# Depthwise convolution: the taps of two of eight channel groups as ScalarE products and GpSimd sums; all input products of the second block in three parts

## The chip, the cores and the metric

One Trainium2 chip, of which the program uses one core. The metric is the device time of one execution in microseconds (us). The engines of the core go by these names: PE is TensorE (PEld its weight loads), DVE is VectorE, ACT is ScalarE, POOL is GpSimd, SP is SyncE, which issues the DMAs. Each engine works through its own list of instructions in order and waits on semaphores for the others.

## The reference

The model has two blocks on 256 tokens of 2048 channels, all in fp32. The change lies in the second block, in its convolution branch:

```python
def conv_group(u, conv_dw_w, conv_dw_b, conv_ln_g, conv_ln_b):
    a, gate = jnp.split(u, 2, axis=-1)
    h = a * jax.nn.sigmoid(gate)
    h = lax.conv_general_dilated(
        h, conv_dw_w[:, None, :].astype(h.dtype), window_strides=(1,),
        padding=[(CONV_K - 1, 0)], dimension_numbers=("NWC", "WIO", "NWC"),
        feature_group_count=CONV_CH) + conv_dw_b
    h = layer_norm(h, conv_ln_g, conv_ln_b)
    return jax.nn.silu(h)

def second_block(x, ...):
    xn = rms_norm(x, norm1_g)
    proj = xn @ w_in + b_in
    # conv_in, q, k, v are slices of proj
    conv_out = conv_group(conv_in, ...)
    attn_out = swa_group(q, k, v, ...)
    x = x + jnp.concatenate([conv_out, attn_out], axis=-1) @ w_out
    ...
```

CONV_CH is 1024 and CONV_K is 31: every channel is convolved along the tokens with its own 31 taps. On the chip a channel is a partition, so the 1024 channels are 8 groups of 128, and a group is 31 taps over a tile of 128 x 256.

## The kernel before

The program is one long list in Python order; a scheduler then sets the order on each engine from its own estimate of when things are ready, so instructions of neighbouring steps stand interleaved.

Products with weights are done in three parts. A weight tile of 512 KB (128 x 1024, ring of 4, name `wr`) comes by DMA; ACT writes its rounded copy `wh` (`wsplit`, L422), DVE subtracts that to get the rest `wl` (L423), both in rings of 3; PE then multiplies wh by the high part of the activation, wh by its low part, and wl by its high part (`three`, L456, L459, L460). A group of 256 output columns is four weight tiles, 96 matmuls of 256 columns (`proj`). For the groups in `N32 = (6, 7)`, that is the last two of the eight convolution inputs, `proj32` (L478) is used instead: the weight tile stays in fp32, ACT scales it in 16 pieces of 128 x 256 (L486), and PE multiplies it with the residual `hT` itself in fp32 (L490), 32 matmuls that the trace shows as 64 records.

The order of the stage in the program is: `conv_in(0)` and `conv_in(1)` (product, tanh gate, and the gated input `hp` of a group, L829 to L833), the product for k and v, four products for q, then eight rounds, each with one more `conv_in` (groups 2 to 7 in the first six) and one attention unit (scores `ps_sc`, softmax on DVE and ACT, transposes `ps_pt`, output `ps_o`, result in `mixed`). After each of these steps `tap(n)` takes up to n taps off a list. A tap is one DVE instruction, co = hp shifted by k, times a weight per channel, plus co (L825; the first tap of a group, with the bias, is L823). Then come the output products of the attention half (`out_half(i, 1)`, eight times 48 matmuls `ps_out`; the last two of them are held behind the mean), with the taps that are left and the scaling of `hT` by the last norm (L873) between. The mean over the channels (`ps_mu`, L882) needs all eight groups of co; the layer norm follows, then the convolution half of the output product.

`hp` and `co` are slices of one tile, which the trace calls `cq`. `ag` is the product of a `conv_in` after its scaling (L402), `q_s` that of a q product. POOL has no instruction in this stage; its first are in the top-k that comes later (L971, L1001).

Of the kernel before, what the change touches and what calls it, by code (L numbers as in the profile page):

```python
# [9 lines left out]
F32 = mybir.dt.float32  # L10
# [4 lines left out]
AF = mybir.ActivationFunctionType  # L15
OP = mybir.AluOpType
# [3 lines left out]
P = 128  # L20
T = 256
# [16 lines left out]
UL = 126  # L38
UB = (6, 4)
VPACE, UPACE, UR = False, True, 4  # L40
N32 = (6, 7)
VR, VB, VLAG = 6, 3, 2
TAPS = (20, 20, 6)
CF = 2
# [154 lines left out]
def body(ctx: ExitStack, tc: tile.TileContext, a, out):  # L199
    nc = tc.nc  # L200
    V, S, G, PE = nc.vector, nc.scalar, nc.gpsimd, nc.tensor
# [40 lines left out]
    def right(stack, name, bufs=1):  # L242
        return stack.enter_context(tc.tile_pool(name=name, bufs=bufs, side="right", reuse_waits="tile"))
# [6 lines left out]
    tm = right(p0, "tm", 2)  # L250
# [3 lines left out]
    def const(name, dtype=F32, pool=rc):  # L254
        shape = list(a[name].shape)
        t = pool.tile(shape, dtype, name="c_" + name)
        nc.sync.dma_start(t, a[name])
        return t
# [96 lines left out]
    def cut(t, o, *shape):  # L355
        n = int(np.prod(shape))
        v = t[:, o:o + n]
        return v.rearrange("p (a b) -> p a b", a=shape[0]) if len(shape) == 2 else v

    def tmp(name, tag, dtype=F32):  # L360
        return tm.tile([P, T], dtype, tag=tag, name=name)
# [37 lines left out]
    def scaled(ps, rr, name):  # L399

        t = tm.tile([P, 512], F32, tag="td", name=name, bufs=3)
        V.tensor_tensor(t.rearrange("p (a b) -> p a b", a=2), ps.rearrange("p (a b) -> p a b", a=2),  # L402
                        twice(rr), OP.mult)
        return t

    def scaled2(ps, rr, name):
        t = total(ps, name)
        t3 = t.rearrange("p (a b) -> p a b", a=2)
        V.tensor_tensor(t3, t3, twice(rr), OP.mult)
        return t  # L410
# [233 lines left out]
    for i in range(4):  # L644
# [14 lines left out]
    for i in range(8):  # L659
        gs = []  # L660
        for name, tag, o, act_in in (("ga", "ta", 0, "w_ga"), ("gb", "tb", 16, "w_gb")):
            t = scaled2(proj2(act_in, i, u), r1, name)
# [4 lines left out]
        t = total(proj2("w_oa", i, ab, kt=2), "ya")  # L667
        for j in range(2):
            V.tensor_tensor(gs[j], gs[j], t[:, j * T:(j + 1) * T], OP.mult)
        t = total(proj2("w_ob", i, ab, kt=2, c0=8), "yb")  # L670
# [32 lines left out]
    for i, shift in ((1, 0.0), (0, 0.25)):  # L703
        k = tmp("an_k", "ta")
# [43 lines left out]
    for gi, n in enumerate(GROUPS):  # L748
        f = cut(slot("ff", F32R), 0, 8, 2 * T)
        for i in range(n):  # L750
            ps = scaled2(proj2("w_up", up0 + i, u), r2, "up")
            cs = []
            for j in range(2):
                ch = 44 * j + up0 + i
                s = ps[:, j * T:(j + 1) * T]
                t = tmp("ff_t%d" % j, "t" + "ab"[j])
# [17 lines left out]
    cw_2 = const("cw_2")  # L774
    cb_2 = const("cb_2")
# [7 lines left out]
    hp = cut(cq, 0, 8, T + 30)  # L783
    co = cut(cq, 2288, 8, T)
# [31 lines left out]
    V.memset(hp[:, :, 0:30], 0.0)  # L816
    taps = []

    def tap(n):
        for _ in range(min(n, len(taps))):  # L820
            i, k = taps.pop(0)
            if k == 0:
                V.tensor_scalar(co[:, i], hp[:, i, 0:T], cw_2[:, i, 0:1], cb_2[:, i:i + 1], OP.mult, OP.add)  # L823
            else:
                V.scalar_tensor_tensor(co[:, i], hp[:, i, k:k + T], cw_2[:, i, k:k + 1], co[:, i],  # L825
                                       OP.mult, OP.add)

    def conv_in(i):
        ps = scaled(proj32("w_in2", i, hT, g_both) if i in N32 else proj("w_in2", i, u), r3, "ag")  # L829
        S.activation(ps[:, T:2 * T], ps[:, T:2 * T], AF.Tanh, bias=hb_in2[:, 2 * i + 1:2 * i + 2], scale=0.5)  # L830
        S.activation(ps[:, 0:T], ps[:, 0:T], AF.Identity, bias=hb_in2[:, 2 * i:2 * i + 1], scale=0.5)
        V.scalar_tensor_tensor(hp[:, i, 30:], ps[:, T:2 * T], 1.0, ps[:, 0:T], OP.add, OP.mult)
        taps.extend((i, k) for k in range(31))  # L833

    for i in range(CF):
        conv_in(i)
        tap(TAPS[2])

    src = scaled(proj("w_in2", 8, u), r3, "kv_s")
# [4 lines left out]
    for tt in range(2):  # L844
        PE.transpose(pt[:, tt * P:(tt + 1) * P], vT[:, tt * P:(tt + 1) * P], ident)
    S.activation(vtok[:, :, :P], pt[:, :T].rearrange("p (a b) -> p a b", a=2), AF.Copy)
    tap(TAPS[2])
    for i in range(4):
        src = scaled(proj("w_in2", 9 + i, u), r3, "q_s")
# [21 lines left out]
    for i in range(8):  # L871
# [5 lines left out]
            out_half(i, 1)  # L877
        tap(TAPS[1])
    tap(len(taps))
    pm = ptp.tile([P, 512], F32, tag="tp", name="ps_mu")  # L880
    for c in range(8):
        mean = PE.matmul(pm[:, :T], onesD, co[:, c], start=c == 0, stop=c == 7)  # L882
# [11 lines left out]
    for c in range(8):  # L894
        V.tensor_tensor(co[:, c], co[:, c], r, OP.mult)
        t = tmp("ln_t", "ta")
# [161 lines left out]
    for h in range(8):  # L1058
# [11 lines left out]
        for tt in range(2):  # L1070
            S.activation(sub[:, tt * T:(tt + 1) * T], pk[:, tt * T:(tt + 1) * T], AF.Copy,
                         scale=r4t[:, tt:tt + 1])
# [260 lines left out]
```

## Time and profile before

| | us |
|---|---|
| median of 3 runs | 3003.82 (3000.06 to 3008.96) |
| the profiled execution | 3007.65 |
| its span | 3005.9 |
| PE busy in the span | 2934.2 (98%) |
| DVE busy | 2399.6 (80%) |
| ACT busy | 1570.0 (52%) |
| POOL busy | 857.2 (29%) |

A profile is one execution, taken by the hardware profiler. A busy share is a mean over stages with different limits, so the rows below cut the span into the stretches around the convolution, from 1385 to 1612 us. An instruction's duration holds some time in which the next one already runs, so of a row of equal instructions the time divided by their count is the better price. The idle time in front of a group of instructions is given with the instruction that ended it. PEclk is the granted clock of TensorE, as a share of full speed (2.4 GHz).

### The profile page before, as it was taken

The numbers are of one execution on the slowest core, as the hardware profiler recorded it, in microseconds if no ns is written. First come the engines' busy times: TensorE is split into PE (matmuls) and PEld (weight loads), VectorE is DVE, ScalarE is ACT, GpSimd is POOL, SyncE is SP. The second block draws the span as 40 slices with busy tenths as digits, with TensorE's granted clock in tenths as the row PEclk, the third lists the DMA queues.
The fourth block names the chain that finished last, engine by engine and source line by source line (L and its number), as shares of the span: only waits on it lengthen the run. The fifth ranks groups of instructions, "written<-read, shape, count | busy, mean of one in ns | idle before, by whom it ended". The sixth has DMA issues, their size and how long they took to land.

```text
span 3005.9 us, 49957 instructions
## 1 busy us (share of the span) xinstructions
PE 2934.2 (98%) x18472; PEld 2620.7 (87%) x18472; DVE 2399.6 (80%) x4392; ACT 1570.0 (52%) x2312; POOL 857.2 (29%) x670
## 2 busy tenths in 40 slices
PE   8999999999999999999989989999999999999999
PEld 7888888888888888878979989999999888888887
DVE  6567666777777676778997788999987988999998
ACT  5565555554545454556565535555555554444444
POOL 0000000000000000000000155555554897777776
PEclk9999999999999999999999999999999999999999
DMA  6446565655665656544434679999999338999998
GB/s 222 155 141 185 189 189 189 190 183 189 189 190 189 189 183 195 187 157 155 148 101 151 231 242 316 325 325 323 323 314 317 112 139 319 331 336 333 332 340 311
DMA packets 211142, 686.35 MB, mean 228 GB/s; under 512 B 29264, under 2 KB 47056, under 8 KB 210512
## 3 DMA queue, kind: packets, MB, share of 16 engines
q1 hardware_dynamic: 169776, 523.15, 52.8%
q0 software_dynamic: 41120, 160.01, 15.6%
q8 instruction: 144, 2.36, 0.3%
q14 instruction: 102, 0.84, 0.1%
HBM read 677.41 MB, written 5.64 MB: 227 GB/s over the span
## 4 chain that ended last, share of the span: by engine, by line
PE 71%; DVE 9%; issue 7%; POOL 7%; DMA 4%; ACT 2%; POOLq 0%; DVEq 0%; SPq 0%; ACTq 0%
PE ps_w_up L443 11%; PE ps_w_up L445 6%; PE ps_dn L443 5%; POOL vrows L1020 5%; PE ps_u L460 3%; PE ps_u L456 3%; PE ps_u L459 3%; DMA urows<-in_u_rows,ex 3%; PE ps_dn L445 3%; PE y L1305 2%; PE y L1304 2%; PE y L1303 2%; PE ps_w_ga L443 2%; PE ps_w_cv L443 2%; PE ps_w_gb L443 2%
## 5 line engine op out<-in xcount | busy, mean ns | idle before, releaser
L423 DVE TENSOR_TENSOR wl<-wr,wh 128x1024 fp32r<-128x1024 f32 x572 | 699.9, 1225 | 358.4 <-ACT wh L422 357.8
L422 ACT ACTIVATE wh<-wr 128x1024 fp32r<-128x1024 f32 x572 | 605.3, 1059 | 672.7 <-PE ps_dn L443 117.8
L971 POOL TENSOR_TENSOR tk_c<-tk_v 128x256 f32<-128x256 f32 x16 | 12.1, 758 | 1714.8 <-DVE tk_v L963 1714.4
L1020 POOL DMA_INDIRECT vrows<-in_v_rows,ex x256 | 382.9, 1496 | 134.7 <-DVE yg L1272 74.8
L460 PE MATMUL ps_u<-u_a,ul 128*128 128x256 f32 x1408 | 401.2, 285 | 15.5 <-DVE ul L423 14.1
L459 PE MATMUL ps_u<-u_a,uh 128*128 128x256 f32 x1408 | 397.8, 283 | 0.0
L456 PE MATMUL ps_u<-u_a,uh 128*128 128x256 f32 x1408 | 397.7, 282 | 0.0
L422 ACT ACTIVATE uh<-ur 128x512 fp32r<-128x512 f32 (+1 forms) x384 | 226.2, 597 | 240.5 <-DMA ur<-in_u_dense 86.7
L443 PE MATMUL ps_w_up<-u_a,wh 128*128 128x512 f32 x968 | 342.8, 393 | 0.0
L1020 POOL DMA_INDIRECT urows<-in_u_rows,ex x228 | 268.4, 1177 | 213.3 <-PE ps_u L460 129.7
L1288 ACT ACTIVATE vhi<-vraw 128x1472 fp32r<-128x1472 f32 x128 | 184.0, 1438 | 264.4 <-PE y L1305 252.5
L1305 PE MATMUL y<-vhi,al 128*128 128x512 f32 (+1 forms) x768 | 298.5, 389 | 0.7 <-DVE al L1296 0.5
L1303 PE MATMUL y<-vhi,ah 128*128 128x512 f32 (+1 forms) x768 | 295.3, 385 | 3.5 <-ACT ah L1295 3.5
L1304 PE MATMUL y<-vlo,ah 128*128 128x512 f32 (+1 forms) x768 | 297.9, 388 | 0.1
L460 PEld LDWEIGHTS ps_u<-u_a,ul 128*128 128x128 f32 x1408 | 266.1, 189 | 23.2 <-DVE ul L423 21.7
L445 PE MATMUL ps_w_up<-u_a,wl 128*128 128x256 f32 x968 | 270.4, 279 | 0.0
L459 PEld LDWEIGHTS ps_u<-u_a,uh 128*128 128x128 f32 x1408 | 265.9, 189 | 0.0
L456 PEld LDWEIGHTS ps_u<-u_a,uh 128*128 128x128 f32 x1408 | 265.8, 189 | 0.0
L423 DVE TENSOR_TENSOR ul<-ur,uh 128x512 fp32r<-128x512 f32 (+1 forms) x384 | 245.6, 662 | 18.8 <-ACT uh L422 15.4
L443 PE MATMUL ps_dn<-ff,wh 128*128 128x512 f32 x704 | 248.0, 395 | 4.9 <-DVE ff L286 3.4
L1291 DVE TENSOR_TENSOR vlo<-vraw,vhi 128x1472 fp32r<-128x1472 f32 x128 | 216.1, 1688 | 42.5 <-ACT vhi L1288 42.5
L443 PEld LDWEIGHTS ps_w_up<-u_a,wh 128*128 128x128 f32 x968 | 181.4, 187 | 43.5
(395 smaller groups left out, 7244.0 us busy)
## 6 DMA issues: line engine op xcount, KB each, us to landing
vraw<-in_v_dense SPq DMA_DIRECT2D x128, 736.0 KB
wr<-in_w_up SPq DMA_DIRECT2D x176, 512.0 KB
ur<-in_u_dense SPq DMA_DIRECT2D x256, 256.0 KB
wr<-in_w_dn SPq DMA_DIRECT2D x88, 512.0 KB
ur<-in_u_dense SPq DMA_DIRECT2D x128, 192.0 KB
wr<-in_w_in SPq DMA_DIRECT2D x44, 512.0 KB
wr<-in_w_cv SPq DMA_DIRECT2D x32, 512.0 KB
wr<-in_w_ga SPq DMA_DIRECT2D x32, 512.0 KB
```

Source lines behind the costliest of these rows:

```text
L422: S.activation(hi, raw, AF.Copy)
L423: low.append(V.tensor_tensor(lo, raw, hi.bitcast(F32), OP.subtract))
L443: PE.matmul(ps[:, j], hi[:, s], x[:, c0 + k, 0:2 * T], start=first and k == 0, stop=False, skip_group_check=True)
L445: PE.matmul(ps[:, j, T:], lo[:, s], x[:, c0 + k, 0:T], start=False, stop=last and k == KC - 1, skip_group_check=True)
L456: m = PE.matmul(o, wh, xh, start=start, stop=False, skip_group_check=True)
L459: PE.matmul(o, wh, xl, start=False, stop=False, skip_group_check=True)
L460: return PE.matmul(o, wl, xh, start=False, stop=stop, skip_group_check=True)
L1020: g = G.indirect_dma_start(out=v, out_offset=None, in_=a[name], in_offset=bass.IndirectOffsetOnAxis(ap=ex[:, tt, s:s + 1], axis=0))
L1291: vlo.append(V.tensor_tensor(lo, raw, hi.bitcast(F32), OP.subtract))
L1303: PE.matmul(o, st, hi[:, c:c + n], start=e2 == 0, stop=False, skip_group_check=True)
L1304: PE.matmul(o, st, lo[:, c:c + n], start=False, stop=False, skip_group_check=True)
L1305: mm = PE.matmul(o, sl, hi[:, c:c + n], start=False, stop=e2 == P - 1, skip_group_check=True)
```

## The change

`N32` becomes empty, so that groups 6 and 7 go through `proj` in three parts as the others do. The taps of groups 0 and 3 go to a list of their own, `ptaps`; each call of `tap` takes up to four off it. Such a tap is a product on ACT (hp shifted, times the channel's weight, into a tile `cv_p` of which there are two) and an addition on POOL (co plus that tile, into co); the first tap is one ACT instruction that writes co with the bias.

```diff
-N32 = (6, 7)
+N32 = ()
+POOLC, PT = (0, 3), 4
...
+    ptaps = []
+
+    def pool_tap():
+
+        i, k = ptaps.pop(0)
+        src, w = hp[:, i, k:k + T], cw_2[:, i, k:k + 1]
+        if k == 0:
+            S.activation(co[:, i], src, AF.Identity, bias=cb_2[:, i:i + 1], scale=w)
+        else:
+            t = tm.tile([P, T], F32, name="cv_p", bufs=2)
+            S.activation(t, src, AF.Copy, scale=w)
+            G.tensor_tensor(co[:, i], co[:, i], t, OP.add)
+
     def tap(n):
+        for _ in range(min(PT, len(ptaps))):
+            pool_tap()
         for _ in range(min(n, len(taps))):
...
-        taps.extend((i, k) for k in range(31))
+        (ptaps if i in POOLC else taps).extend((i, k) for k in range(31))
...
     tap(len(taps))
+    while ptaps:
+        pool_tap()
```

Line numbers behind the change are higher by 1 up to L817 of before, by 16 from L820 on and by 18 from L880 on: L423 and L424 are now `wh` and `wl`, L830 and L831 the product and the addition of a moved tap, L841 a tap on DVE, L846 and L847 the tanh and bias of `ag`.

The first place is ACT's list from the tanh of `conv_in(0)` on. Before, it goes on with weight tiles until `conv_in(1)`:

```order
L830 ACT_TABLE_LOAD
L830 ACTIVATE ag<-ag,hb_in_12494 128x256
L831 ACTIVATE ag<-ag,hb_in_12494 128x256
L422 ACTIVATE wh<-wr 128x1024 x4
L830 ACTIVATE ag<-ag,hb_in_12494 128x256
L831 ACTIVATE ag<-ag,hb_in_12494 128x256
L422 ACTIVATE wh<-wr 128x1024 x4
L841 ACTIVATE v_s<-kv_s,c_b_in_12477 128x256
```

Now the products stand between the weight tiles, on the same engine:

```order
L846 ACT_TABLE_LOAD
L846 ACTIVATE ag<-ag,hb_in_12494 128x256
L847 ACTIVATE ag<-ag,hb_in_12494 128x256
L423 ACTIVATE wh<-wr 128x1024
L827 ACTIVATE cq_12493<-cq_12493,c_cb_12481,c_cw_12479 128x256
L830 ACTIVATE cv_p<-cq_12493,c_cw_12479 128x256 x3
L423 ACTIVATE wh<-wr 128x1024
L830 ACTIVATE cv_p<-cq_12493,c_cw_12479 128x256 x5
L423 ACTIVATE wh<-wr 128x1024
L830 ACTIVATE cv_p<-cq_12493,c_cw_12479 128x256 x5
L423 ACTIVATE wh<-wr 128x1024
L846 ACTIVATE ag<-ag,hb_in_12494 128x256
```

All 30 products of group 0 stand ahead of `v_s`, that is within the eight weight tiles of `conv_in(1)` and of k and v.

The second place is ACT's list from the `ag` of `conv_in(3)` on. Before:

```order
L830 ACTIVATE ag<-ag,hb_in_12494 128x256
L831 ACTIVATE ag<-ag,hb_in_12494 128x256
L577 ACTIVATE mixed<-ps_o 128x2x128
L553 ACTIVATE at_p,at_den<-ps_sc,at_nm 128x256
L549 ACTIVATE at_es<-at_es 128x4
L553 ACTIVATE at_p,at_den<-ps_sc,at_nm 128x256 x3
L422 ACTIVATE wh<-wr 128x1024
L558 ACTIVATE at_p<-at_p,at_den 128x256 x4
L422 ACTIVATE wh<-wr 128x1024 x3
```

Now:

```order
L846 ACTIVATE ag<-ag,hb_in_12494 128x256
L847 ACTIVATE ag<-ag,hb_in_12494 128x256
L578 ACTIVATE mixed<-ps_o 128x2x128
L827 ACTIVATE cq_12493<-cq_12493,c_cb_12481,c_cw_12479 128x256
L830 ACTIVATE cv_p<-cq_12493,c_cw_12479 128x256 x6
L423 ACTIVATE wh<-wr 128x1024
L550 ACTIVATE at_es<-at_es 128x4
L554 ACTIVATE at_p,at_den<-ps_sc,at_nm 128x256 x4
L830 ACTIVATE cv_p<-cq_12493,c_cw_12479 128x256
L423 ACTIVATE wh<-wr 128x1024
L559 ACTIVATE at_p<-at_p,at_den 128x256 x4
L423 ACTIVATE wh<-wr 128x1024
```

The exponentials of the softmax (`at_p` from `ps_sc`) and the weight tiles stand behind six products there; of the 30 of group 3, 26 stand ahead of the `ag` of `conv_in(5)`.

The third place is DVE's list from the `ag` of the last `conv_in` on (`at_m`, `at_nm`, `at_es` belong to the softmax of an attention unit). Before, taps, scalings of `hT` and, soon, weight tiles for the output product:

```order
L402 TENSOR_TENSOR ag<-ps_w_in_14450,r_12511 128x512
L825 SCALAR_TENSOR_TENSOR cq_12493<-cq_12493,c_cw_12479 128x256
L873 SCALAR_TENSOR_TENSOR hT<-hT,c_g_fin,s_12497 128x256
L825 SCALAR_TENSOR_TENSOR cq_12493<-cq_12493,c_cw_12479 128x256
L873 SCALAR_TENSOR_TENSOR hT<-hT,c_g_fin,s_12497 128x256
L832 SCALAR_TENSOR_TENSOR cq_12493<-ag 128x256
L578 TENSOR_TENSOR mixed<-ps_o,mixed 128x2x128
L825 SCALAR_TENSOR_TENSOR cq_12493<-cq_12493,c_cw_12479 128x256
L543 TENSOR_REDUCE at_m<-ps_sc 128x4
L825 SCALAR_TENSOR_TENSOR cq_12493<-cq_12493,c_cw_12479 128x256
L544 TENSOR_TENSOR at_m<-at_m,c_sink_12489 128x4
L423 TENSOR_TENSOR wl<-wr,wh 128x1024
```

Now taps alone, in longer rows; the next `wl` is 40 rows behind this `ag`:

```order
L403 TENSOR_TENSOR ag<-ps_w_in_14631,r_12511 128x512
L841 SCALAR_TENSOR_TENSOR cq_12493<-cq_12493,c_cw_12479 128x256 x3
L848 SCALAR_TENSOR_TENSOR cq_12493<-ag 128x256
L841 SCALAR_TENSOR_TENSOR cq_12493<-cq_12493,c_cw_12479 128x256 x3
L579 TENSOR_TENSOR mixed<-ps_o,mixed 128x2x128
L841 SCALAR_TENSOR_TENSOR cq_12493<-cq_12493,c_cw_12479 128x256
L544 TENSOR_REDUCE at_m<-ps_sc 128x4
L841 SCALAR_TENSOR_TENSOR cq_12493<-cq_12493,c_cw_12479 128x256
L545 TENSOR_TENSOR at_m<-at_m,c_sink_12489 128x4
L841 SCALAR_TENSOR_TENSOR cq_12493<-cq_12493,c_cw_12479 128x256 x2
L547 TENSOR_SCALAR at_nm<-at_m 128x4
L549 TENSOR_TENSOR at_es<-c_sink_12489,at_m 128x4
```

The scalings of `hT` have moved to the front of the stage, around `conv_in(0)`, since no fp32 product reads `hT` any more. Behind the mean the lists of DVE and POOL are the same as before.

## Rows read from the trace of the kernel before

**Rows 1.** Busy time by stretch: us, then PE, PEld, DVE, ACT, POOL, clock, DMA.

```profile
1385.60:1421.90 36.30, 36.11 (x298) 35.75 (x297) 34.77 (x64) 20.06 (x26) 0.00 (x0) 1.00 0.55 175
1421.90:1476.10 54.20, 54.18 (x408) 50.67 (x408) 49.95 (x85) 29.87 (x41) 0.00 (x0) 1.00 0.50 157
...
1489.30:1553.40 64.10, 63.20 (x414) 54.42 (x410) 63.84 (x163) 41.29 (x111) 0.00 (x0) 1.00 0.37 116
1553.40:1584.50 31.10, 23.63 (x142) 17.63 (x141) 28.82 (x72) 18.13 (x53) 0.00 (x0) 0.84 0.29 87
1584.50:1612.30 27.80, 27.80 (x231) 27.73 (x230) 24.67 (x42) 10.04 (x11) 0.00 (x0) 1.00 0.53 168
...
1577.00:1581.00 4.00, 4.00 (x21) 4.00 (x20) 4.00 (x12) 1.76 (x5) 0.00 (x0) 0.50 0.89 255
```

**Rows 2.** Groups of instructions, 1370 to 1640 us: busy, mean ns, idle ahead.

```profile
L825 DVE SCALAR_TENSOR_TENSOR cq<-cq,c_cw 128x256 f32<-128x256 f32 x240 | 105.5, 476 | 0.8
L423 DVE TENSOR_TENSOR wl<-wr,wh 128x1024 fp32r<-128x1024 f32 x62 | 75.6, 1219 | 9.0 <-ACT wh L422 8.9
...
L486 ACT ACTIVATE w<-w,c_g 128x256 f32<-128x256 f32 x32 | 13.5, 504 | 3.3 <-PE ps_pt L564 1.7 <-DMA w<-in_w_in 1.6
```

**Rows 3.** DVE in order of time: start us, us, operation.

```profile
1397.29 0.68 DVE L402 TENSOR_TENSOR ag<-ps_w_in,r 128x512 f32<-128x512 f32 x1
...
1402.40 2.06 DVE L825 SCALAR_TENSOR_TENSOR cq<-cq,c_cw 128x256 f32<-128x256 f32 x5
1404.38 1.22 DVE L423 TENSOR_TENSOR wl<-wr,wh 128x1024 fp32r<-128x1024 f32 x1
1405.52 1.67 DVE L825 SCALAR_TENSOR_TENSOR cq<-cq,c_cw 128x256 f32<-128x256 f32 x4
...
1409.03 0.68 DVE L402 TENSOR_TENSOR kv_s<-ps_w_in,r 128x512 f32<-128x512 f32 x1
...
1503.72 0.68 DVE L402 TENSOR_TENSOR ag<-ps_w_in,r 128x512 f32<-128x512 f32 x1
...
1518.84 0.69 DVE L402 TENSOR_TENSOR ag<-ps_w_in,r 128x512 f32<-128x512 f32 x1
...
1536.17 0.68 DVE L402 TENSOR_TENSOR ag<-ps_w_in,r 128x512 f32<-128x512 f32 x1
...
1553.36 0.68 DVE L402 TENSOR_TENSOR ag<-ps_w_in,r 128x512 f32<-128x512 f32 x1
```

**Rows 4.** POOL's additions in the later top-k, and DVE beside them.

```profile
L971 POOL TENSOR_TENSOR tk_c<-tk_v 128x256 f32<-128x256 f32 x16 | 12.1, 758 | 1714.8 <-DVE tk_v L963 1714.4 <-issue 0.3
...
1706.44 0.62 POOL L971 TENSOR_TENSOR tk_c<-tk_v 128x256 f32<-128x256 f32 x1 [2.99 <-DVE tk_v L963]
1706.55 1.60 DVE L423 TENSOR_TENSOR wl<-wr,wh 128x1024 fp32r<-128x1024 f32 x1
...
1837.43 1.71 DVE L423 TENSOR_TENSOR ul<-ur,uh 128x512 fp32r<-128x512 f32 x2
1838.08 0.63 POOL L971 TENSOR_TENSOR tk_c<-tk_v 128x256 f32<-128x256 f32 x1
...
1848.96 0.68 DVE L423 TENSOR_TENSOR ul<-ur,uh 128x512 fp32r<-128x512 f32 x1
```

**Rows 5.** A weight tile on ACT and DVE, with the idle time ahead and its end.

```profile
1382.58 1.06 ACT L422 ACTIVATE wh<-wr 128x1024 fp32r<-128x1024 f32 x1 [1.82 <-PE ps_w_in L459]
...
1383.67 1.23 DVE L423 TENSOR_TENSOR wl<-wr,wh 128x1024 fp32r<-128x1024 f32 x1 [1.18 <-ACT wh L422]
...
1385.58 0.69 DVE L402 TENSOR_TENSOR ag<-ps_w_in,r 128x512 f32<-128x512 f32 x1 [0.68 <-PE ps_w_in L460]
```

**Rows 6.** PE's longest idle times in the stage, and in the chain, the mean.

```profile
1559.58 0.38 PE L460 MATMUL ps_out<-mixed,wl 128*128 128x256 f32 x1 [2.45 <-DVE wl L423]
...
1576.07 0.58 PE L460 MATMUL ps_out<-mixed,wl 128*128 128x256 f32 x1 [2.77 <-DVE wl L423]
...
1612.28 3.02 PE ps_mu L882 x14
```

## The prediction

> **What bounds the kernel now.** I read the page first, then the busy times by stretch, the instruction groups, and DVE's and PE's timelines. By stretch the stage falls into five parts, and POOL has no work in any of them [rows 1]. E (1385.6 to 1421.9, first `ag` to first `q_s`) and Q (to 1476.1, the q products) have PE busy throughout. R (1489.3 to 1553.4, the `ag` of groups 3 to 7) has PE at 63.2 and DVE at 63.8 of 64.1 us. F (to 1584.5, from the last `ag` to the last `mixed`) has PE at only 23.6 of 31.1 us and a clock of 0.84. O (to 1612.3, the output products up to the mean) has PE full again. So PE sets the time except in F, where it waits twice, 2.45 and 2.77 us, for DVE's `wl` [rows 6]. DVE is the engine next in line: its 240 taps alone are 105.5 us [rows 2].
>
> DVE's list can be added up. Five taps have 1.98 us from the start of the first to the next row, so a tap is 0.40, and a `wl` 1.14, since the row behind it starts that much later [rows 3]. With 0.60 for a row of 512 columns, 0.36 for one of 256, 1.05 for the softmax maximum and 0.09 for a small one, R's rows of before give 14.5 + 15.2 + 17.4 + 17.8 = 64.9 us against the 64.0 from one `ag` to the last [rows 1, 3]. The sum holds, and DVE, not PE, is what R's length follows; its fp32 groups, though, leave PE little room either.
>
> PE's price is in the same view: from `ag` to `kv_s` are 96 matmuls in 11.74 us, 0.122 each [rows 3]. In O, 226 matmuls stand between the last `ps_o` and the seven last `ps_mu`, and 27.8 us for them is 0.123 each [rows 1].
>
> **Part 1: groups 6 and 7 in three parts.** Their rounds run from 1518.84 to 1536.17 and to 1553.36, 17.3 and 17.2 us [rows 3]. The round ahead of them, an ordinary group with its attention unit, runs from 1503.72, 15.1 us with PE busy. On PE that is worth 2 x 2.1 = 4.2 us. DVE gets 8 more `wl`, 9.1 us; ACT loses 32 pieces (13.5 us [rows 2]) and gets 8 `wh` of 1.06. The scalings of `hT` move ahead: 10 of the 16 fall into E.
>
> **Part 2: 62 taps leave DVE.** They are 24.8 us there. ACT gets 62 products; the nearest row is the scaling of a 128 x 256 piece, 13.5/32 = 0.42 each [rows 2], 26 us. POOL gets 60 additions of 0.63 us by the nearest row (a 128 x 256 addition, mean 0.76 because some wait) [rows 4].
>
> What these cost DVE is the disputed price. Where a POOL addition meets a DVE instruction with both inputs in SBUF, the trace shows one waiting for the other: a `wl` that meets a 0.62 us addition takes 1.60 instead of 1.22, two `ul` take 1.71 where 0.60 + 0.68 is usual [rows 4]. So an addition takes about 0.43 us from DVE. Taps, `wl` and scalings of `hT` are all of that kind. The bounds are 0 (the addition falls beside rows that read PSUM, as `ag` does, or beside idle time) and 0.63 (all of it lost). I take 0.43: a tap that moves gives DVE 0.40 and takes 0.43.
>
> The Trainium skill has a rule on this, SBUF — State Buffer, section "Who interferes with whom": a VectorE instruction with two SBUF inputs and a GpSimd instruction that reads SBUF lock each other out, and the second blocks until the first has finished. By that rule each addition would cost its whole 0.63 us, 6 us more per group of 30 than by the row; the trace agrees on the lock and shows a smaller price, and I stay with the row.
>
> **Sum by stretch.** A weight tile is ready only a little ahead. ACT starts `wh` when PE has left the tile three back, and `wl` follows at 1383.67 to 1384.90 for the tile that PE takes up one tile time (2.9 us) after the group's end at about 1385.3 [rows 5]. That is 3.3 us of slack, and what DVE or ACT is late beyond it, PE loses.
>
> E: by the order, DVE has 23 taps instead of 39 (-6.4) and 10 scalings (+4.0), so 31.6 us instead of 34.0. All 30 additions of group 0 fall in here: 30 x 0.43 = 12.9, of which I let 2 stand beside rows that read PSUM. 42.5 less 3.3 is 39.2, against 36.3: 2.9 late. But ACT's list puts all 30 products ahead of `v_s`, with two buffers, so the eighth `wh` waits for 28 additions. Up to its `wl` DVE has 19.0 us of rows, with 28 x 0.43 = 12.0 it ends at 1416.6; before it ended at 1408.3. 8.3 less 3.3 is 5.0. I take +5; 0 if the additions hide, 10 if neither slack nor cover helps.
>
> Q: DVE has 42.0 us of rows instead of 47.9, PE its 54.2. Nothing changes, and what PE lost in E is not won back.
>
> R: DVE's rows now are 14.1 + 14.0 + 17.8 + 12.0 = 57.9, PE's 4 x 15.1 = 60.4: without locks 3.6 shorter than before. The 30 additions of group 3 add 12.9, less 2: 68.8, less the slack 65.5. Against 64.0 that is +1.5 to +4.8; I take +3 (-3.6 to +8). ACT is no better: 26 products stand in two rounds, ahead of exponentials and weight tiles.
>
> F: DVE's rows from the last `ag` to the last `mixed` are 31.2 us instead of 29.5 (53 taps instead of 34, 3 `wl` instead of 5, no scalings): +1.7. There is no POOL work left in F.
>
> O: PE's order now has 276 matmuls behind the last `ps_o` instead of 226, because the 50 that filled F before (62 then, 12 now) have moved behind it: 50 x 0.122 = +6.1. They wait for nothing in O that they can avoid, since PE is full there. With PE idler in F the clock may stay low longer; it was 0.50, the lower of the two levels (1.2 GHz), from 1577 to 1581, behind PE's two waits [rows 1, 6]. That is 0 to +3, taken as 0.
>
> Behind the mean the lists are the same, and shift as a whole. The sum is 5 + 3 + 1.7 + 6.1 = 15.8 us over the profiled execution's 3007.65, or 3023.5; that execution lies 3.8 above the median of the runs, so against the median 3003.82 + 15.8 = 3019.6.
>
> **Rivals.**
> A, the additions hide: they fall beside ACT's and PE's waits and cost DVE nothing. For it: in each round DVE has 2 us of rows that read PSUM, and the lock seen was shorter than the addition. Against it: DVE is over 95% busy in E and R [rows 1]. Then E is 0, R -3.6, F and O stay: +4.2, 3008.
>
> B, faster: DVE's sum decides as a whole, not the order. 24.8 - 9.1 = 15.7 us go from DVE, and if the additions are free and DVE's shorter list lets PE fill F, the stage loses that: 3003.8 - 15.7 = 2988. For it: DVE is the releaser in F [rows 6]. Against it: F's own rows on DVE are longer than before. It decides if F comes out shorter than 31 us. The Trainium skill (Perfetto Trace Analysis, "Optimizing Scalar/DVE Operations") says that offloading work to Scalar or GPSIMD may make sense where DVE is saturated, and adds that the shared read port may undo it. No run here shows the gain.
>
> C, ACT is blocked: with two buffers, a product waits for the addition two back, and an addition waits for a DVE row (0.40 to 1.14) each time, about 1.1 us a tap. ACT's rows in the two rounds of group 3 are then about 19 and 20 us (other work 10.9 and 10.4, products 8 and 9.5) against PE's 15.1, and E takes 28 x 1.1 = 31 us to the eighth tile, from 1389.3 to 1420: E +10, R +8, with F, O and the clock's 3: 28.8, 3033. It decides if `wh`, not `wl`, is what PE waits for.
>
> **How the numbers follow.** Forecast 0.52 (3010 to 3029), A 0.22, C 0.19, B 0.07. A measurement of this kernel tells 0.3%, 9 us, from no change. Slower by more than that, above 3012.8, are C and most of the forecast: 0.65. Within are A and the forecast's low end: 0.28. Faster is B: 0.07. The range, 3003 to 3034, leaves out B, the lower part of A and the upper part of C.
>
> **What would show it.** In the profile after: POOL's additions with a mean well over 0.63 us, and taps or `wl` beside them with means above 0.48 and 1.22; PE idle in E ahead of the tiles of `conv_in(1)`, k and v, and in the rounds of groups 3 to 5, ended by `wl` or `wh`; from the last `ag` to the last `mixed` 31 us or more with PE under half busy; 33 to 34 us from there to the mean. Wrong would be POOL additions of 0.63 with DVE rows at their old lengths (A), or a mean that is reached earlier than 227 us after the first `ag` (B).

## The result, and the profile after

The changed kernel took 3038.02 us (median of 4 runs, 3031.41 to 3041.03) against 3004.18 for the kernel before: a ratio of 1.0105, 95% interval 1.0092 to 1.0119; the medians lie 33.8 us apart. Its profiled execution took 3037.46 us with a span of 3035.7. The forecast was 3019.6, its range ended at 3034.

The stretches of after, in the columns of [rows 1] (us, then PE, PEld, DVE, ACT, POOL, clock, DMA):

```profile
1385.70:1435.90 50.20, 39.06 (x295) 37.41 (x293) 42.56 (x59) 32.95 (x57) 27.61 (x30) 0.93 0.40 127
1435.90:1490.80 54.90, 54.77 (x410) 50.89 (x410) 44.72 (x69) 29.70 (x41) 0.00 (x0) 1.00 0.49 155
1504.00:1576.60 72.60, 64.55 (x475) 56.97 (x472) 68.80 (x130) 49.41 (x118) 26.86 (x30) 0.91 0.35 109
1576.60:1612.30 35.70, 21.47 (x95) 12.08 (x93) 30.91 (x79) 16.44 (x51) 0.00 (x0) 0.62 0.13 41
1612.30:1646.00 33.70, 33.70 (x281) 33.65 (x280) 22.30 (x29) 12.50 (x13) 0.00 (x0) 1.00 0.50 161
```

These are E, Q, R, F and O. Against [rows 1] E is 13.9 longer, Q 0.7, R 8.5, F 4.6, O 5.9: 33.6 us. The two profiled executions differ by less, 29.8 us, because behind the mean, where the lists are the same, after took 1386.5 us and before 1390.5; over the profiled executions below this part lies between 1386.1 and 1394.1, so a change is read from its stretches and not from the total of one execution.

In E no engine is full: the busiest, DVE, has 42.6 of 50.2 us. In R it has 68.8 of 72.6. That points to a hand-over between engines, and the timeline of after on DVE, ACT and POOL shows it (start us, us, operation, idle ahead and what ended it):

```profile
1412.09 5.03 POOL L831 TENSOR_TENSOR cq<-cq,cv_p 128x256 f32<-128x256 f32 x5 [0.27 <-ACT cv_p L830]
...
1414.70 3.71 DVE L841 SCALAR_TENSOR_TENSOR cq<-cq,c_cw 128x256 f32<-128x256 f32 x4
1415.40 0.51 ACT L830 ACTIVATE cv_p<-cq,c_cw 128x256 f32<-128x256 f32 x1 [1.17 <-POOL cq L831]
1415.81 1.04 ACT L423 ACTIVATE wh<-wr 128x1024 fp32r<-128x1024 f32 x1
...
1418.33 1.75 DVE L424 TENSOR_TENSOR wl<-wr,wh 128x1024 fp32r<-128x1024 f32 x1
...
1420.86 0.68 DVE L403 TENSOR_TENSOR kv_s<-ps_w_in,r 128x512 f32<-128x512 f32 x1
1421.10 1.04 ACT L423 ACTIVATE wh<-wr 128x1024 fp32r<-128x1024 f32 x1
1421.46 1.33 DVE L841 SCALAR_TENSOR_TENSOR cq<-cq,c_cw 128x256 f32<-128x256 f32 x2
```

Four taps beside additions are 3.6 us from their start to the next row, 0.91 apiece instead of 0.40; a `wl` is 1.75; five additions are 5.03, 1.0 apiece; a product waits 1.17 us for an addition; and from one `wh` to the next it is 5.3 us, where a tile lasts PE 2.9. The row `kv_s` comes at 1420.86, 35.1 us behind the first `ag`; before, it was 23.5 behind [rows 3, 5]. PE was done with k and v at about 1417.4, but in DVE's list four taps, a `wl` and one more tap stand ahead of `kv_s`. The groups of 1370 to 1660 us (busy, mean ns, idle ahead) have the same in sums:

```profile
L841 DVE SCALAR_TENSOR_TENSOR cq<-cq,c_cw 128x256 f32<-128x256 f32 x180 | 92.4, 538 | 1.6
L424 DVE TENSOR_TENSOR wl<-wr,wh 128x1024 fp32r<-128x1024 f32 x67 | 86.0, 1283 | 20.7 <-ACT wh L423 20.7
L831 POOL TENSOR_TENSOR cq<-cq,cv_p 128x256 f32<-128x256 f32 x60 | 54.5, 908 | 1496.2 <-ACT cv_p L830 1492.6
L830 ACT ACTIVATE cv_p<-cq,c_cw 128x256 f32<-128x256 f32 x60 | 29.1, 503 | 18.5 <-POOL cq L831 18.4
```

DVE now stands idle 20.7 us ahead of `wl`, for `wh`; before, it was 9.0 between 1370 and 1640 [rows 2]. PE's waits, in E, then in R, then in F (us in total, times, longest):

```profile
PE ps_qn L811 <- ACT qk_q L809: 6.0, 1, 6.0
PE ps_w_in L461 <- DVE wl L424: 4.4, 3, 2.2
PE ps_w_in L457 <- ACT wh L423: 0.8, 1, 0.8
...
PE ps_o L572 <- ACT at_pt L567: 7.8, 2, 4.3
...
PE ps_out L461 <- DVE wl L424: 5.1, 1, 5.1
PE ps_sc L533 <- ACT at_p L554: 5.0, 1, 5.0
PE ps_sc L533 <- DVE cq L841: 3.1, 1, 3.1
```

PE's longest waits in E and R are not for weight tiles but at small matmuls: `ps_qn` (the norm of k, from `kv_s` by way of `qk_q`) and `ps_o` (from the softmax). Behind the waits at both the granted clock was 0.50 (1.2 GHz):

```profile
1424.00:1426.00 2.00, 2.00 (x10) 1.88 (x9) 1.59 (x4) 1.77 (x3) 0.00 (x0) 0.50 0.46 113
...
1525.00:1528.00 3.00, 3.00 (x13) 1.69 (x11) 1.47 (x4) 1.22 (x3) 1.45 (x2) 0.50 0.56 164
```

### The profile page after: what moved, and what is told of

It is laid out like the page before. It is cut to its first block, busy times and chain, and to the rows that moved or that the text cites. A ratio compares the mean times of both kernels' runs of the same rounds, so it can differ in the third digit from the quotient of the medians.

```text
span 3035.7 us, 50204 instructions
## 1 busy us (share of the span) xinstructions
PE 2941.3 (97%) x18536; PEld 2623.8 (86%) x18536; DVE 2407.1 (79%) x4338; ACT 1590.2 (52%) x2350; POOL 918.2 (30%) x730
## 4 chain that ended last, share of the span: by engine, by line
PE 80%; DVE 9%; DMA 4%; issue 3%; POOL 2%; ACT 2%; DVEq 0%; POOLq 0%; SPq 0%; ACTq 0%
PE ps_w_up L444 11%; PE ps_w_up L446 5%; PE y L1323 5%; PE y L1322 5%; PE y L1321 5%; PE ps_dn L444 5%; PE ps_u L461 3%; PE ps_u L457 3%; PE ps_u L460 3%; PE ps_dn L446 3%; PE ps_w_ga L444 2%; PE ps_w_cv L444 2%; PE ps_w_gb L444 2%; PE ps_w_mix L444 2%; PE ps_a L1243 2%
## 5 line engine op out<-in xcount | busy, mean ns | idle before, releaser
L424 DVE TENSOR_TENSOR wl<-wr,wh 128x1024 fp32r<-128x1024 f32 x580 | 713.8, 1232 | 371.0 <-ACT wh L423 370.3
L423 ACT ACTIVATE wh<-wr 128x1024 fp32r<-128x1024 f32 x580 | 613.6, 1058 | 671.8 <-PE ps_dn L444 117.9
L831 POOL TENSOR_TENSOR cq<-cq,cv_p 128x256 f32<-128x256 f32 x60 | 54.5, 908 | 1496.2 <-ACT cv_p L830 1492.6
L1038 POOL DMA_INDIRECT vrows<-in_v_rows,ex x256 | 394.5, 1541 | 120.4 <-DVE yg L1290 58.7
L423 ACT ACTIVATE uh<-ur 128x512 fp32r<-128x512 f32 (+1 forms) x384 | 224.7, 596 | 242.5 <-DMA ur<-in_u_dense 98.6
L424 DVE TENSOR_TENSOR ul<-ur,uh 128x512 fp32r<-128x512 f32 (+1 forms) x384 | 245.5, 663 | 23.5 <-ACT uh L423 22.9
```

The costliest lines, as they stand in the source:

```text
L423: S.activation(hi, raw, AF.Copy)
L424: low.append(V.tensor_tensor(lo, raw, hi.bitcast(F32), OP.subtract))
L1038: g = G.indirect_dma_start(out=v, out_offset=None, in_=a[name], in_offset=bass.IndirectOffsetOnAxis(ap=ex[:, tt, s:s + 1], axis=0))
```

## The experiments

Two theories after the result. **Hand-over**: in E and R the lock between POOL's additions and DVE, and ACT's wait for POOL ahead of `wh`, lose the time; **order**: in F and O it is lost by the new order, whatever POOL does. The lock is the name here for what the prediction describes: a DVE row with two inputs in SBUF and a POOL instruction hold each other up. The table gives each run's stretches between rows on DVE: E from the first `ag` to the first `q_s`, Q with the round behind it to the `ag` of group 3, R to the last `ag`, F + O to the first row that uses the mean.

| run | E | Q + round | R | F + O | ratio (95%) |
|---|---|---|---|---|---|
| before | 36.3 | 67.5 | 64.0 | 62.0 | |
| after | 50.1 | 68.2 | 72.5 | 72.6 | 1.0105 (1.0092, 1.0119) |
| e1 part 1 alone | 36.1 | 67.0 | 60.2 | 69.6 | 1.0005 (0.9996, 1.0014) |
| e2 part 2 alone | 50.3 | 68.2 | 77.6 | 58.0 | 1.0070 (1.0057, 1.0084) |
| e4 sums, no products | 45.0 | 67.8 | 69.6 | 72.2 | 1.0084 (1.0068, 1.0099) |
| e6 memset for addition | 36.8 | 68.2 | 60.4 | 70.9 | 1.0018 (1.0007, 1.0028) |
| e7 copy for addition | 43.9 | 68.2 | 65.6 | 72.4 | 1.0070 (1.0054, 1.0086) |
| e3 buffers 12 and 4 | 42.8 | 70.8 | 71.4 | 72.2 | 1.0090 (1.0074, 1.0106) |
| e11 four buffers | 47.6 | 67.8 | 72.1 | 70.5 | 1.0098 (1.0083, 1.0114) |
| e15 norm of k later | 49.7 | 68.7 | 73.8 | 69.3 | 1.0102 (1.0085, 1.0119) |
| e17 k and v later | 47.3 | 69.6 | 73.1 | 69.3 | 1.0099 (1.0082, 1.0116) |
| e9 31 taps a unit | 36.1 | 67.0 | 79.6 | 65.8 | 1.0056 (1.0043, 1.0069) |
| e10 16 taps a step | 48.6 | 67.9 | 85.2 | 56.4 | 1.0097 (1.0083, 1.0112) |
| e13 before, 4 taps | 36.3 | 67.5 | 63.9 | 59.5 | 0.9997 (0.9988, 1.0006) |
| e14 part 1, 12 taps | 36.1 | 67.0 | 59.3 | 68.1 | 1.0010 (1.0001, 1.0019) |
| e16 additions in Q | 36.4 | 76.5 | 59.3 | 68.2 | 1.0036 (1.0026, 1.0046) |

**e1_three and e2_pool: each part by itself.**

```diff
e1: -POOLC, PT = (0, 3), 4
    +POOLC, PT = (), 4
e2: -N32 = ()
    +N32 = (6, 7)
```

> Part 1 alone: groups 6 and 7 in three parts, all taps on DVE. Theory (order): the growth behind the last `ag` comes from this part alone, since its order has 19 output matmuls between the last input product and the last `ps_o` (before 62, after 12) and 269 behind it (before 226, after 276): E 36 and Q 54 as before, F 34 to 36 (before 31.1, after 35.7), O 33 (226 at 27.8, so 269 at 33.1), and R, where DVE gets 8 more `wl` for 32 scalings moved away, 61 to 65. Sum +5 to +10 us: 3009 to 3014. Rival (both parts together): F and O only grow because DVE comes late out of R; then F + O stay near 59 and the time is 3000 to 3005.

> Part 2 alone: taps of groups 0 and 3 on ACT and POOL, groups 6 and 7 in fp32 as before. Theory (hand-over): E and R lose what they lose in the full change, E +12 to +15 and R +5 to +9; behind the last `ag` the order has 80 output matmuls as filling and 208 behind it, so F + O are 0 to 5 shorter than before. Sum +14 to +22: 3018 to 3026. Rival (DVE's load): 24.8 us of taps leave DVE and no weight tile comes, so R and F gain what E loses and the time is within 5 us of before.

Part 1 alone makes F + O 7.6 longer, and that without a POOL instruction: the rival, that F and O only grow behind a late DVE, falls. But R comes out 3.8 shorter, at 60.2, near PE's own length of 4 x 15.1, where 61 to 65 was expected, and the time is the same as before within 0.14%, not 5 to 10 us over. Part 2 alone has the whole loss of E; its R lost 13.6, more than the 5 to 9 expected, and F + O is 4.0 shorter, as the order's 80 matmuls of filling said (output products that PE can do while it waits for an attention unit).

By the ratios part 1 costs 0.05%, part 2 0.70% and both together 1.05%. So most of the change is part 2's loss, and about 0.3%, some 9 us, come only with both. F + O shows most of that: the parts alone give +7.6 and -4.0, both together +10.6, since 12 matmuls of filling are left there instead of 19 or 80.

**e4_sums, e6_memset, e7_copy: what of the pair costs.** The lists of PE, DVE and ACT of e6 and e7 are those of the full change.

```diff
-            G.tensor_tensor(co[:, i], co[:, i], t, OP.add)
e4: +        G.tensor_tensor(co[:, i], co[:, i], src, OP.add)   # and no ACT product
e6: +        G.memset(t, 0.0)
e7: +        G.tensor_copy(co[:, i], t)
```

> The changed kernel with the 60 products on ACT left out: POOL adds hp shifted by k, without its weight, straight into co. The lock between POOL's additions and DVE stays, ACT has no buffer to wait for. Theory (lock and buffers together): E is what DVE's rows need, 31.6 us and 30 additions of 0.53, less 3.3 of slack: 44 to 46, some 5 less than the 50.1 of the full change; no `wl` waits more than 1 us for `wh`; total 3024 to 3032. Rival (lock alone): the waits for `wh` only follow from the lock, E stays 49 to 51, and the total within 3 us of the full change. Rival (ACT alone): without products E goes back to 36 to 38.

> The changed kernel with POOL's 60 additions replaced by a memset of the product's tile, so the sums of groups 0 and 3 are left out; the instruction lists of PE, DVE and ACT are word for word those of the full change, and so are the hand-overs from ACT to POOL and back through two buffers. POOL reads nothing. Theory (lock): taps go back to 0.40 to 0.42 us a piece, a product no longer waits 1.17 us, E is 36 to 39 and R 60 to 65; F and O keep what the order makes of them (35 and 33.7); total 3009 to 3016. Rival (ACT's load and the hand-over): the products themselves and their two buffers hold `wh` up; E stays over 45 and the total over 3028.

> The full change with POOL's addition replaced by a copy of the product into co, so the sums of groups 0 and 3 are left out; all instruction lists but POOL's kind are word for word those of the full change. POOL reads one tile instead of two. Theory (any read of SBUF by POOL locks out DVE's two-input rows): taps beside copies take 0.8 to 0.9 us apiece as with additions, E over 43, R over 67, total 15 to 34 over before. Rival (only POOL's two-input operations lock): taps stay 0.40 to 0.48, E 36 to 38, R 60 to 61, total 4 to 8 over before as with the memset.

Busy times of E and R, in the columns of [rows 1], of e6:

```profile
1383.90:1420.70 36.80, 35.75 (x293) 35.26 (x293) 33.37 (x58) 32.21 (x57) 9.37 (x30) 1.00 0.55 173
1488.90:1549.30 60.40, 59.29 (x474) 53.77 (x471) 58.80 (x130) 48.38 (x118) 9.36 (x30) 1.00 0.41 132
```

of e4:

```profile
1385.70:1430.70 45.00, 37.67 (x297) 36.97 (x296) 44.14 (x60) 20.18 (x27) 28.73 (x30) 0.92 0.46 142
1498.50:1568.10 69.60, 62.62 (x472) 56.04 (x471) 68.55 (x130) 36.73 (x88) 27.84 (x30) 0.93 0.36 114
```

and of e7:

```profile
1386.10:1430.00 43.90, 37.65 (x293) 36.80 (x292) 34.66 (x59) 32.70 (x57) 16.39 (x30) 0.92 0.47 145
1498.20:1563.80 65.60, 60.70 (x474) 54.60 (x471) 60.70 (x129) 48.87 (x118) 16.81 (x30) 0.97 0.38 121
```

With memsets all 60 products, buffers and waits are still there, and E is 36.8 and R 60.4: PE's own lengths. ACT's 32 us of rows in E hide. So it is the addition itself that costs, and e6's first theory holds. A memset differs from it in more than one way: it reads nothing, it lasts 0.31 us instead of 0.91, and it writes `cv_p` and not `co`. The next two runs take DVE's loss and ACT's apart.

In e4, with ACT's products gone, DVE is full (44.1 of 45.0, 68.6 of 69.6): the lock makes DVE the bound, and E and R are 8.2 and 9.2 over e6. E came out at 45.0 as its first theory said, and not at either rival's length. In e7 it is the other way round: copies cost DVE 1.3 us in E and 1.9 in R, hardly anything, and yet E and R are 7.1 and 5.2 over e6. There ACT's rows wait for POOL, and `wh` with them:

```profile
1404.44 1.22 DVE L424 TENSOR_TENSOR wl<-wr,wh 128x1024 fp32r<-128x1024 f32 x1
1404.48 3.59 POOL L831 COPY cq<-cv_p 128x256 f32<-128x256 f32 x5 [0.75 <-ACT cv_p L830]
1405.58 2.23 DVE L841 SCALAR_TENSOR_TENSOR cq<-cq,c_cw 128x256 f32<-128x256 f32 x4
1405.95 1.59 ACT L830 ACTIVATE cv_p<-cq,c_cw 128x256 f32<-128x256 f32 x3 [1.20 <-POOL cq L831]
```

Five copies take 0.72 apiece here; the shortest of the run is 0.40.

So there are two losses, DVE's time and ACT's pace, each enough for 5 to 9 us a group, and the full change has both: 13.3 and 12.2 over e6, less than their sum, as they overlap. Of e7's two theories neither held as written: the taps stayed near their length (0.51 in the mean of E, against 0.48 with memsets and 0.71 with additions), as the second said, and the time was lost all the same, as the first said. F + O stays at 70.9 to 72.4 in all three, so it is the order's, as in e1.

PE's rows show a part of E and R that neither theory names. For the same matmuls (within two) PE is busy 39.06 us in E of after and 35.75 in that of e6, and 64.55 against 59.29 in R: some 3 and 5 us of the 13.3 and 12.2 are matmuls at the lower clock behind PE's waits, and only the rest is idle time. It comes with the two losses; no run here has these waits at full clock, so what it adds to the time by itself is not shown.

**e3_ring and e11_ring4: more buffers.**

```diff
-            t = tm.tile([P, T], F32, name="cv_p", bufs=2)
+            n = 4 if i == 0 else 4     # e3: 12 if i == 0 else 4
+            j = k % n
+            o = 7152 + T * j if j < 4 else 4336 + T * (j - 4)
+            t = cq[:, o:o + T]
```

> The full change with more buffers for the products: 12 for group 0 and 4 for group 3, cut from a part of `cq` that is free at the time, in place of two. The order then puts 10 of group 0's 30 additions into Q. Theory (lock and buffers): the two buffers add what the full change has over the run without products, 5.1 us in E and 2.9 in R; this goes, and additions in Q cost nothing there, so E is 41 to 45, R 69 to 71, F and O as in the full change, total 22 to 27 us over before: 3027 to 3032. No `wl` waits over 1.5 us for `wh` in E. Rival (the buffers only show the lock): E over 48, total within 4 us of the full change's 34 over before.

> The full change with four buffers for the products instead of two, in a free part of `cq`, for groups 0 and 3 alike; result unchanged, and all 30 products of group 0 stand ahead of `v_s` in ACT's list, as in the full change. Theory A (the pair of buffers is what holds ACT up): with twice the buffers most of the 8.0 us that the products add to the run without them goes: E 45 to 47, R 69 to 71, total 25 to 29 over before. Theory B (POOL's pace of about 1 us an addition holds ACT up, whatever the buffers, since 28 products stand ahead of the last `wh`): two more buffers are two additions, 2 us a group: E 47.5 to 49, R 70 to 72, total 29 to 32 over.

e3 is no clean test: eight of the twelve buffers lie where q is stored, so some of the products from the 16th on wait for the q products and overwrite part of q, from which the scores are then computed. With half the additions in Q it shows E at 42.8 and Q + round 2.6 longer. e11 is clean: E is 47.6 and R 72.1, 2.5 and 0.4 less than with two buffers, near theory B's lengths and over theory A's. But B's reason is only half of it. ACT's waits for POOL do shrink, from 10.6 to 7.4 us in E and from 7.8 to 1.4 in R. DVE's rows grow in turn, to 44.5 and 70.6 us, so that DVE is nearly full, as in e4:

```profile
1385.30:1432.90 47.60, 40.43 (x295) 39.62 (x294) 44.54 (x59) 33.37 (x57) 29.65 (x30) 0.89 0.41 134
1500.70:1572.80 72.10, 63.52 (x474) 57.11 (x471) 70.61 (x130) 48.90 (x118) 28.41 (x30) 0.91 0.36 110
```

So the pair of buffers does hold ACT up, as rival C of the prediction said, but what more buffers win at ACT is for the most part lost again at the lock. In E POOL's pace of 0.99 us an addition (29.65/30) holds ACT up besides.

**e15_knorm and e17_kvlate: is the wait at `ps_qn` the loss?** In e15 the call of `qk_norm` for k stands behind the first q product, in e17 v's transpose too. (e12, an earlier run of e15's kernel, gave 1.0101.)

```diff
-    qk_norm(src[:, :T], 16, 1, 1, [kT[:, 0]])
+    kv = src
...
         src = scaled(proj("w_in2", 9 + i, u), r3, "q_s")
+        if i == 0:
+            qk_norm(kv[:, :T], 16, 1, 1, [kT[:, 0]])
```

> The full change with the norm and the rotation of k written behind the first q product once more (k's `ps_qn` 75 matmul rows later in PE's list), for its profile. Theory (in-order PE): the wait at `ps_qn` is under 1.5 us instead of 6.0, and from the first `ag` to group 2's it is 99 to 101.5 us instead of 105.05; total 27 to 31 over before. Rival (weight tiles): PE waits for `wl` or `wh` right behind instead, the stretch is 103 to 105 us, total 32 to 35 over.

> The full change with both readers of `kv_s` on PE, v's transpose and the norm of k, written behind the first q product (in PE's list `ps_qn` 74 and `ps_vt` 73 rows later). Theory A (PE's list): PE goes on with the first q tiles while DVE is late at `kv_s`; from the first `ag` to group 2's it is 99 to 101.5 us instead of 105.05, total 27 to 31 over before. Theory B (the whole of DVE's and ACT's lists is late): PE, at the end of k and v at 1417.4, would take up the first q tile when its `wl` ends at 1420.1 in the full change and the second at 1423.9, against 1423.4 for `ps_qn`, so 2.5 us at the most are won, PE waits 2 to 4 us for `wl` there, and the stretch is 102.5 to 105 us, total 31 to 35 over.

In e15 the wait moved to the other reader of `kv_s`, v's transpose, PE's longest wait from the start of E to the end of Q, while its waits for `wl` stayed as in after:

```profile
PE ps_vt L861 <- ACT v_s L857: 4.7, 1, 4.7
PE ps_w_in L461 <- DVE wl L424: 4.4, 3, 2.2
```

and from the first `ag` to group 2's it was 104.5 us instead of 105.05. In e17 both are gone and the stretch is 104.4, within theory B's range: E is 2.8 shorter, but a wait of 2.7 us at `ps_rot`, for `kv_s` again, stands in Q instead. So moving the small matmuls wins nothing that the times show (1.0102 and 1.0099 against 1.0105): the next one that needs `kv_s` waits in their place, since DVE's and ACT's lists are late as a whole.

**e9_taps31, e10_taps16, e13_taps4, e14_taps12: does filling set F + O?** All without POOL; e13 keeps N32 = (6, 7), the others have it empty. The numbers of `TAPS` say how many taps are taken behind an attention unit, behind an output group, and behind a step ahead of the rounds.

```diff
-TAPS = (20, 20, 6)
+TAPS = (31, 20, 6)     # e9; e10: (31, 31, 16); e13: (20, 4, 6); e14: (12, 4, 6)
```

> Part 1 alone again (three parts for groups 6 and 7, all taps on DVE), with up to 31 taps instead of 20 taken after each attention unit, so that the order has 67 output matmuls between the last input product and the last `ps_o` (19 in part 1 alone, 62 before). Theory (filling): F + O fall from 69.6 back to 61 to 64 while R keeps the 60 to 61 of part 1: total 3 us under to 1 us over before, and PE busy over 26 us in F. Rival (DVE's rows): the filling needs `wl`, which DVE has to do between the same taps, so F grows by what O loses; F + O over 67 and the total 1 to 6 over before.

> As the run with 31 taps a unit, and also 31 instead of 20 behind each output group and 16 instead of 6 behind each step ahead of the rounds, so taps move into E and Q where DVE has 2 and 6 us to spare; 88 output matmuls in F. Theory (filling): E 36 to 37, Q 54 to 55, R 60 to 62, F + O 57 to 62: total 2 to 8 under before. Rival (DVE has no room ahead of F): E or R come out 3 or more longer, since taps stand ahead of weight tiles there, and the total is over before.

> The kernel before with up to 4 taps instead of 20 taken behind each output group (no tap leaves DVE, groups 6 and 7 in fp32): DVE's rows up to the last `ag` are the same, and 84 output matmuls stand in F where before had 62, 6 `wl` there instead of 5. Theory (filling, where DVE has room for it): E, Q and R as before, F 29 to 31, O 26.5 to 28.5 by DVE's 25.8 and PE's 204 matmuls, F + O 56 to 59.5 instead of 62: total 2 to 6 under before. Rival (DVE's rows): 22 more matmuls need a `wl` more in F, F grows by what O loses: within 2 us of before.

> Part 1 with all taps on DVE, up to 12 taps a unit and 4 behind each output group: by rows of before DVE has 36.5 in E, 50.6 in Q, 59.6 in R, 27.2 in F and 36.6 in O, and 90 output matmuls stand in F. Theory (each stretch as long as the larger of DVE's rows and PE's): E 36, Q 54, R 60.4, F 27.5 to 30, O 36.5 to 38 by DVE: total 3 under to 1 over before. Rival (filling alone): O is PE's 198 matmuls, 25 to 28, and the total 8 to 12 under before.

By the output matmuls that stand in F, F + O is 72.6 for 12 (after), 69.6 for 19 (e1), 65.8 for 67 (e9), 62.0 for 62 (before), 59.5 for 84 (e13), 58.0 for 80 (e2) and 56.4 for 88 (e10), but 68.1 for 90 (e14), where PE waits 11.6 us at the mean for taps that DVE still has to do. So filling shortens F + O as long as DVE's rows are not in the way, and taps that make room by going ahead cost more in the earlier stretches than they win in F + O: e9's R, with 75.7 us of DVE rows, took 79.6, and e10's E 48.6 with 46.8. The gains expected of e9 and e10 failed at DVE's sum; e10's rival held, while e9's rival had its loss in F and not in R. e14's theory, the larger of DVE's rows and PE's, held against its rival: F + O is 68.1, where it had 64 to 68, and the time is 0.10% over before, where the rival had 8 to 12 us under. e13 reaches the mean 2.6 us earlier than before and cannot be told from it in time; no version beat the kernel before.

F of e10 in the columns of [rows 1]:

```profile
1587.30:1616.20 28.90, 22.56 (x155) 16.20 (x154) 26.82 (x65) 17.28 (x45) 0.00 (x0) 1.00 0.26 86
```

and four pieces of after, in F and behind it:

```profile
1580.00:1585.00 5.00, 0.39 (x4) 0.18 (x2) 5.00 (x14) 1.67 (x8) 0.00 (x0) 0.98 0.01 2
1585.00:1590.00 5.00, 4.40 (x19) 2.89 (x21) 4.70 (x14) 3.14 (x8) 0.00 (x0) 0.50 0.00 0
...
1606.00:1612.00 6.00, 6.00 (x24) 3.83 (x24) 4.95 (x9) 2.79 (x6) 0.00 (x0) 0.50 0.74 230
1612.00:1616.00 4.00, 4.00 (x33) 3.77 (x32) 3.08 (x6) 1.45 (x2) 0.00 (x0) 0.98 0.13 52
```

In after the clock fell to 0.50 (1.2 GHz) behind PE's wait of 5.0 us and stayed there for the rest of F, so that the chain of scores, transposes and outputs itself ran at half speed; with e10's filling it stayed at 1.00.

**e16_inq: additions where DVE has room.** e14 with group 0 on ACT and POOL, its first tap held back to Q by a bias that is read from the first q product (the calls of `tap` ahead of the q products take none of its taps):

```diff
-POOLC, PT = (0, 3), 4
+POOLC, PT = (0,), 8
+            V.scalar_tensor_tensor(b0, src[:, 0:1], 0.0, cb_2[:, 0:1], OP.mult, OP.add)
...
-            S.activation(co[:, i], src, AF.Identity, bias=cb_2[:, i:i + 1], scale=w)
+            S.activation(co[:, i], src, AF.Identity, bias=b0, scale=w)
```

> The run with 12 taps a unit (groups 6 and 7 in three parts), but with group 0's taps on ACT and POOL, and their first tap made to wait for the first q product, so that 28 of the 30 products and all additions fall behind the start of Q, the most of them into its first two products. DVE has 40.7 us of rows in Q instead of 50.6 and PE 54, so it has room for 30 additions of 0.36. Theory (a full DVE is what makes additions dear): E 36 to 37, additions of 0.70 to 0.85, Q and the round behind it 67 to 71 instead of 67.0, since ACT has some 30 us of rows in two products of 27; R, F and O as in that run; total 0 to 7 over it, 3 to 10 over before. Rival (an addition takes about 1 us and holds ACT up whatever DVE does): the two products take 40 us, Q and the round 77 or more, total 12 or more over before.

Q + round is 9.5 longer than in e14, near the rival's 77, and the total, 10.8 over before, lies between the two theories. The groups of POOL, and the stretch in which the additions lie:

```profile
L831 POOL TENSOR_TENSOR cq<-cq,cv_p 128x256 f32<-128x256 f32 x30 | 28.0, 933 | 1430.9 <-ACT cq L827 1424.7 <-ACT cv_p L830 4.2 <-POOL cq L831 0.2
...
1422.10:1459.00 36.90, 30.97 (x213) 28.77 (x212) 31.22 (x38) 27.54 (x50) 27.61 (x30) 0.91 0.40 126
```

The additions still took 0.93 with DVE busy 31.2 of 36.9 us, and PE waited 5.9 us at `ps_rot` for `q_s`, a row of DVE's in the chain of a q product. Room in DVE's sum does not help where rows of DVE stand in a chain that PE's list waits for.

## Why the prediction was wrong

**What bounds it, E, Q, R, F, O.** That PE sets the time except in F, and DVE stands next, held. R's DVE rows with locks were put at 68.8 and are 68.8 in the profile after; E's at 42.5 and are 42.6. That they agree to 0.1 is in part luck: by e6 the rows without locks are 33.4 and 58.8 instead of 31.6 and 57.9, and the additions cost 9.2 and 10.0 instead of 10.9. POOL's additions, put at 0.63, are 0.72 at the shortest and 0.91 in the mean, and take 0.31 us (E) and 0.33 (R) of busy time from DVE by the difference to e6, (42.56 - 33.37)/30 and (68.80 - 58.80)/30. The prediction had 0.43 less 2 us of cover a group, that is 0.36.

**The step that failed** is the one from DVE's rows to the stretch: "That is 3.3 us of slack, and what DVE or ACT is late beyond it, PE loses." For E it made 39.2 of 42.5, beside a second count that gave the +5, and for R 65.5 of 68.8. E is 50.2 and R 72.6. Two things were wrong in it.

The slack was not there. E and R each run from one row of DVE's list to another, and all the rows that were added up stand between the two, so 42.5 and 68.8 were the least that E and R could be: +6.2 and +4.8, where the forecast took +5 and +3. e4, with DVE alone as the bound, has them 0.9 and 1.0 *longer* than DVE's rows, not 3.3 shorter. The slack is that of a weight tile; `kv_s`, the softmax and `ps_rot` go through DVE and ACT to small matmuls in PE's list, and e15 and e17 show PE waiting at one or another of them. The second count left out the same: it put the `wl` ahead of `kv_s` 8.3 us late, its end is 11.6 us late in after (34.4 us behind the first `ag` instead of 22.7), and `kv_s` comes as late, so nothing of the 3.3 was given back. (The `wh` of that `wl` stands behind 25 products in after, not behind the 30 that the count took.)

And DVE does not work through its rows without a pause: it idles 7.6 us in E, 6.7 of them for `wh` behind ACT, which is paced by POOL, and 3.8 in R, mostly at rows of the attention units that wait for PE or ACT. 39.2 + 3.3 + 7.6 = 50.1, and 65.5 + 3.3 + 3.8 = 72.6. On PE's side the same time is waits of 11.2 and 8.0 us and matmuls at a clock of 0.50, which the prediction had named for F alone.

**Rival C** described this pace and had 0.19. It was weighed as one that takes the place of the forecast; e4 and e7 show each of the two losses nearly by itself, and the full change has both at once. Its E +10 and R +8 are near the +13.9 and +8.5, its 3033 is nearer than my 3019.6. Its condition, that PE waits for `wh` and not `wl`, was badly put: in E PE waits 0.8 us for `wh`, while DVE waits 6.7, so the pace reaches PE through `wl` and `kv_s`. Its cause, two buffers, is a part of it, but no remedy by itself (e11).

**The lock.** The Trainium skill's rule, SBUF — State Buffer, section "Who interferes with whom", sets POOL instructions that read SBUF against DVE's two-input rows and leaves out those that only write. e6 agrees: beside memsets, which only write, a tap lasts 0.48 us in the mean, as before [rows 2]. For additions the price of a whole instruction comes near where the two alternate: four taps in a row at 0.91 instead of 0.40 pay 0.51 each. Over a stretch an addition costs DVE 0.31 to 0.39 (after, e4 and e11 against e6), while it lasts 0.9 to 1.0. For copies the rule's price does not agree: they read too, last 0.55 in the mean, and cost DVE 0.04 to 0.06.

**Part 1.** R's 3.6 to 4.2 us for PE were right: R is 60.2 in e1 and 60.4 in e6, as the sum of 60.4 had it. O, +6.1 by 50 matmuls, is +5.9. F, +1.7 by DVE's rows, is +4.6: DVE's 31.2 us of rows are 30.9, but F is 35.7, since DVE waits there too (2.9 us for scores of PE's), and PE's chain runs at a clock of 0.62 in the mean. A row of eight score matmuls shows it, in F of after and behind the last `ag`, where the clock was still full:

```profile
1576.90 1.14 PE L533 MATMUL ps_sc<-cq 64*128 64x256 f32 x8
...
1595.54 2.08 PE L533 MATMUL ps_sc<-cq 64*128 64x256 f32 x8 [3.12 <-DVE cq L841]
```

The prediction named 0 to 3 us for the clock and took 0.

**A and B.** A is what e6 has: R 60.4, F + O longer, 1.0018 in all, or 5.4 us against A's 4.2. So it comes true where POOL writes memsets instead of adding. B fell with F at 35.7.

**What would show it.** Most of it came: additions well over 0.63, taps beside them at 0.91 and `wl` at 1.75, PE idle in E for `wl`, F over 31, 33.7 us to the mean. Two signs did not: in R it is the softmax (7.8 us) and not `wl` or `wh` (0.2) that ends PE's idle time, and in F PE is busy 21.5 of 35.7 us, not under half. Those that came fit C as well as the forecast, and could not tell the two apart.

## What to carry to other kernels

A tap moved from DVE to POOL saved 0.40 us of DVE and cost 0.31 to 0.39 there, so the move had next to nothing to win from the start; what it added was a hand-over ACT to POOL to ACT ahead of work that PE needs. Look first at what stands behind the waiting instruction on its engine, and when two mechanisms each explain a loss, ask whether they can come together before giving each its own chance. A slack measured at one kind of tile holds only for waits on that tile: rows that go back to PE in a chain need their own.

## What had not been expected of the hardware

POOL copies that read one tile lengthen DVE's rows by 0.04 to 0.06 us each (34.66 - 33.37 over 30 in E), while they themselves go from 0.40 us at the shortest to 0.72 beside taps: there it is POOL that gives way. With additions both do: a tap goes from 0.40 to 0.91, an addition from 0.72 at the shortest to 1.0.
